# Attention weights turned by VectorE in 32x32 blocks and placed through DRAM, their normalisation on ScalarE

## The chip, the cores and the metric

One core of one Trainium2 chip runs the whole program. The metric is the device time of one execution in microseconds (us), smaller being better. The kernel before takes 1813.17 us (median of three runs, 1809.98 to 1820.33).

## What is computed

Two layers of a model on 256 latent tokens and 256 context tokens, width 2048, all in fp32. The first layer has 16 attention heads and 32 state-space heads beside each other (one input projection, one output projection); the second is a gated short convolution. Each layer is modulated by shift, scale and gate vectors, which are the product of a conditioning vector with a large matrix `ada_w`. The part that the change touches is the attention of one head:

```python
s_lat = jnp.einsum('bqhd,bkhd->bhqk', qr, kb).astype(jnp.float32) * scale + bias.astype(jnp.float32)
s_lat = jnp.where(mask, s_lat, -jnp.inf)
s_ctx = jnp.einsum('bqhd,bkhd->bhqk', qr, k_ctx).astype(jnp.float32) * scale
pr = jax.nn.softmax(jnp.concatenate([s_lat, s_ctx], axis=-1), axis=-1).astype(v.dtype)
return (jnp.einsum('bhqk,bkhd->bqhd', pr[..., :kh * GRID_W], vb)
        + jnp.einsum('bhqk,bkhd->bqhd', pr[..., kh * GRID_W:], v_ctx))
```

With 256 queries and 512 keys a head has 256x512 weights. They come out of the softmax with queries on the partitions, and the product with the values needs them with keys on the partitions, so they have to be turned.

## The kernel before, in words

**Weights.** Nearly all of the time goes into products with weight matrices, which are read from DRAM once. SP's queue loads them in tiles of 512 KB (L379, in `issue`) into five raw buffers, `raw_131` to `raw_135`. ACT casts a tile to its high part wH (L409, `split`), DVE forms the low part wL (L416, `low_part`) and thereby frees the raw buffer, and PE does three products for each tile (L198, `mm`). There are three pairs of wH and wL, so ACT can be three tiles ahead of PE at most, and SP five more. A tile is 24 matmuls of 512 columns in the input projection of keys, queries and the like, and 12 of 512 in the output projection.

**The order.** Python generators describe the work (one per head, per state-space group, per projection). A planner (`Plan`, L38) guesses what each instruction costs and, from the guesses, decides when a generator may issue its next step; every engine then runs its own list strictly in order. A changed cost guess, or a generator that holds a temporary buffer for longer, so moves instructions of other parts on all engines. There are ten temporary buffers of 128x512 (`tmp_104` to `tmp_113`), and a head reserves some with `grow` before it starts.

**An attention head** (`head_gen`, L992; 16 of them). Four DMAs of 64 KB on SP fetch the bias (L998). For each half of the queries (qt = 0, 1) PE forms the scores, one matmul of 128x512; DVE adds the bias and takes the maximum (L1013), ACT takes the exponential with its sum (L1018). DVE then forms the reciprocal of the sum (L1022) and multiplies the weights by it and by 0.5 (L1023). PE turns the weights, four transposes of 128x128 into a PSUM bank (`trans`, L1026 to 1028, through `turn`, L202), and ACT copies the bank to the tile PT (L1050). Four matmuls multiply with the values (L1058), DVE multiplies by the gate (L1062), and a DMA on ACT's queue writes the result to DRAM (L921). The two tiles PT_149 and PT_150 alternate between heads.

**Convolution of the state-space groups.** When the projection for B or C of a group is finished in its PSUM bank, ACT starts the convolution from that bank (L1169), DVE goes on with it, and ACT ends it with an activation (L1178).

**The modulation of the second layer** (`gemv_gen`, L787) is work in the background: 16 vectors of 512, and for each one eight tiles of `ada_w` of 512 KB, loaded by SP among the weights into the same raw buffers when one is to spare, and two multiply-adds on DVE for each (L803). The finished row goes by PE, DVE (L812) and a DMA on ACT's queue to DRAM (L815). When vector 11 is done, the twelve rows are read back by a DMA (L819), turned by PE and copied by DVE (L824); only then can `turn_gen` scale and turn the input of the second layer (L1556, L1568). The first matmul of the second layer needs that.

**The border of the layers.** The output projection ends with a multiply and an add on DVE for every bank (L1531, L1534, giving x1a and x1b); then follow a root mean square, transposes and the scaling, and the second layer's h (L1636 on ACT, L1617 on DVE).

**Completion of DMAs.** Eight completion counters go round among the DMAs of SP and of ACT: a DMA waits until the one eight before it has landed.

In the kernel after, a line from L988 to L1021 stands one line lower, and one behind `head_gen`'s middle nine lines lower: L1169 becomes L1178, L1178 becomes L1187, L1531 becomes L1540, L1534 becomes L1543, L1568 becomes L1577.

Of the kernel before, what the change touches and what calls it, by code (L numbers as in the profile page):

```python
# [11 lines left out]
ALU = mybir.AluOpType  # L12
# [25 lines left out]
class Plan:  # L38
# [32 lines left out]
    def cost(self, e, op, i, ins, outs):  # L71
        n = max(self.size(a) for a in ins + outs)
        if e == "PE":
            n, cols = self.size(outs[0]), outs[0].ap[0][1]
            if i.is_transpose:
                return n / 1.2 + 3, 190
            if ins[0].dtype == F32R:
                return 9 + 0.434 * n, 190
            return 2 * max(55, n / 1.2) * (0.27 if cols == 32 else 0.52 if cols == 64 else 1) + (80 if cols < 128 else 0), 190
        if e == "DVE":  # L80
            if op == "Memset":
                return n * 0.26 + 60, 90
            if op in ("Reciprocal", "TensorReduce"):
                return n * 1.04 + 70, 90
            if len([a for a in ins if self.size(a) >= n]) >= 2 or op == "ISA" or self.psum(ins):
                return n * 1.22 + 70, 90
            return n * 0.6 + 130, 90
        if e == "ACT":
            return n * 0.85 + 150 + (200 if len(outs) > 1 else 0), 100
        if e == "POOL":  # L90
            return (n * 186 if n < 70 else n * 2.4) + 150, 60
        return 60, 0
# [49 lines left out]
def kernel(ctx: ExitStack, tc, x, cx, ada_w, ada_b, w_in, w_out, sc_in, sc_out, rpb, small, const,  # L142
# [7 lines left out]
    V, S, G, T, DMA = nc.vector, nc.scalar, nc.gpsimd, nc.tensor, nc.sync  # L150
    DMA2 = nc.scalar
    plan = Plan()
    E = plan.add

    def st(shape, tag, dt=F32, name=None):
        return sb.tile(list(shape), dt, tag=tag, name=name or tag, bufs=1)
# [11 lines left out]
    def drt(shape, name):  # L168
        return dr.tile(list(shape), F32, name="dram_" + name)
# [3 lines left out]
    free_t = [st([128, 512], f"tmp{k}") for k in range(NTMP)]  # L173
    free_h = [st([128, 256], f"half{k}") for k in range(NHALF)]
    free_b = [pj.tile([128, 512], F32, tag=f"bank{k}", name=f"bank{k}", bufs=1) for k in range(8)]
# [4 lines left out]
    KT, QT, Vt, gt = st([128, 4, 512], "KT"), st([128, 4, 256], "QT"), st([128, 4, 512], "Vt"), st([128, 4, 256], "gt")  # L180
# [7 lines left out]
    def take(pool):  # L188
        b = min(pool, key=lambda a: plan.last[a.tensor.name])
        pool[:] = [a for a in pool if a is not b]  # L190
        return b

    tmp, half, raw_ = (lambda: take(free_t)), (lambda: take(free_h)), (lambda: take(free_r))
    two = lambda ap: ap.rearrange("p (a b) -> p a b", a=2)
    four = lambda ap: ap.rearrange("p (a b) -> p a b", a=4)

    def mm(o, l, r, start, stop):
        E(T.matmul(o, l, r, start=start, stop=stop, skip_group_check=True))  # L198

    def turn(o, i):  # L200
        k = i.shape[0]
        E(T.transpose(o, i, ident if k == 128 else ident[:k, :k]))  # L202
# [132 lines left out]
    def bank():  # L335
        return take(free_b)

    def give(pool, *bs):
        pool.extend(bs)

    W_ = lambda eng, *aps, nb=0: (eng, aps, nb)
# [577 lines left out]
    def put_mix(i, o):  # L919
        yield W_("AQ", o)  # L920
        E(DMA2.dma_start(mixd[i], o))  # L921
        give(free_h, o)
        written.add(i)
# [63 lines left out]
        got.add((key, a))  # L987

    b0 = rpbs[0, :, :]
    s4s = [st([128, 8], f"s4_{k}") for k in range(4)]  # L990

    def head_gen(a, h):  # L992
        hd = 4 * a + h
        bt, s4, P = bias[hd % 2], s4s[hd % 4], PT[hd % 2]
        yield when(lambda: hd < 2 or ("pv", hd - 2) in got)
        yield W_("SP")
        for r in range(4):
            E(DMA.dma_start(bt[64 * (r % 2):64 * (r % 2) + 64, r // 2, :].rearrange("p (a b) -> p a b", a=4),  # L998
                            bass.AP(tensor=b0.tensor, offset=b0.offset + hd * 64 * 320 + (7 - r) * 31 - 61,
                                    ap=[[319, 64], [31, 4], [1, 64]])))  # L1000
        yield W_("DVE", bt)
        bv = bt[:, 0:2, :].rearrange("p q (r c) -> p (q r) c", c=64)
        E(V.tensor_tensor(out=bv, in0=bv, in1=mask.unsqueeze(1).to_broadcast([128, 8, 64]), op=ALU.add))
        sps = {}

        def score(qt):
            ps = bank()
            mm(ps, QT[:, h, qt * 128:(qt + 1) * 128], KT[:, h, :], True, True)
            return ps

        def top(qt, ps):
            sp = sps[qt] = tmp()
            E(V.tensor_tensor_reduce(out=two(sp), in0=two(ps), in1=bt[:, 1:3, :] if qt else bt[:, 0::2, :], scale=1.0,  # L1013
                                     scalar=-3.0e38, op0=ALU.add, op1=ALU.max, accum_out=s4[:, qt:qt + 1]))
            give(free_b, ps)
            E(V.tensor_scalar(out=s4[:, 2 + qt:3 + qt], in0=s4[:, qt:qt + 1], scalar1=-1.0, scalar2=None, op0=ALU.mult))
            yield W_("ACT", sp, s4)
            E(S.activation(sp, sp, AF.Exp, bias=s4[:, 2 + qt:3 + qt], scale=1.0, accum_out=s4[:, 4 + qt:5 + qt]))  # L1018

        def scale_(qt):  # L1020
            sp = sps[qt]  # L1021
            E(V.reciprocal(s4[:, 6 + qt:7 + qt], s4[:, 4 + qt:5 + qt]))  # L1022
            E(V.tensor_scalar(out=sp, in0=sp, scalar1=s4[:, 6 + qt:7 + qt], scalar2=0.5, op0=ALU.mult, op1=ALU.mult))  # L1023

        def trans(qt):
            pt = bank()  # L1026
            for kt in range(4):
                turn(pt[:, kt * 128:(kt + 1) * 128], sps[qt][:, kt * 128:(kt + 1) * 128])
            give(free_t, sps[qt])
            return pt  # L1030

        yield when(lambda: ("K", a) in got and ("Q", a) in got)
        yield ("grow", 2, 0)
        yield W_("PE", KT[:, h, :], QT[:, h, :], nb=1)
        p0 = score(0)
        yield W_("DVE", p0)
        yield from top(0, p0)
        yield W_("PE", nb=1)
        p1 = score(1)
        yield W_("DVE", p1)  # L1040
        yield from top(1, p1)
        yield W_("DVE", sps[0])
        scale_(0)
        yield W_("DVE", sps[1])
        scale_(1)
        for qt in range(2):
            yield W_("PE", sps[qt], nb=1)
            pt = trans(qt)
            yield W_("ACT", pt)
            E(S.copy(P[:, :, qt * 128:(qt + 1) * 128], four(pt)))  # L1050
            give(free_b, pt)
        yield ("cap", 0, 0)
        yield when(lambda: ("V", a) in got and ("G", a) in got)
        yield ("grow", 0, 1)
        yield W_("PE", P, Vt, nb=1)
        po = bank()
        for kt in range(4):
            mm(po[:, :256], Vt[:, kt, h * 128:(h + 1) * 128], P[:, kt, :], kt == 0, kt == 3)  # L1058
        got.add(("pv", hd))
        yield W_("DVE", po)  # L1060
        o = half()
        E(V.tensor_tensor(out=o, in0=po[:, :256], in1=gt[:, h, :], op=ALU.mult))  # L1062
        give(free_b, po)
        attn[0] += 2
        yield from put_mix(hd, o)
# [381 lines left out]
    for h in range(4):  # L1447
        spawn(side, head_gen(0, h))
# [11 lines left out]
    def do_qk(a, nxt):  # L1460
        psQ = banks(2)
        proj(512, "act", psQ, 4)
        spawn(urgent, kq_gen("Q", a, psQ, 2, statq, QT, True), 2)
        psK = banks(4)
        proj(512, "act", psK, nxt)
        spawn(urgent, kq_gen("K", a, psK, 4, statk, KT, True), 4)
        for h in range(4):
            spawn(side, head_gen(a, h))
# [388 lines left out]
```

## Time and profile before

| what | value |
|---|---|
| median of three runs | 1813.17 us (1809.98 to 1820.33) |
| the profiled execution | 1814.06 us, its span 1812.3 us |
| granted clock of TensorE in that execution | 0.999 |
| busy | PE 98%, DVE 69%, ACT 43%, POOL 2% of the span |
| 16 DMA engines, queue q1 (SP's loads) | 63.8% of their span |

The profile is of one execution. "Busy" is the time in which an engine has an instruction running; PE is the matmul engine, DVE is VectorE, ACT is ScalarE, SP is the engine whose queue starts most of the DMAs. A group of instructions in the profile is a line of the kernel with its tiles and shape; "idle before" is how long the engine stood still ahead of such instructions, and what it waited for.

### The profile page before, as it was taken

The numbers are of one execution on the slowest core, as the hardware profiler recorded it, in microseconds if no ns is written. First come the engines' busy times: TensorE is split into PE (matmuls) and PEld (weight loads), VectorE is DVE, ScalarE is ACT, GpSimd is POOL, SyncE is SP. The second block draws the span as 40 slices with busy tenths as digits, with TensorE's granted clock in tenths as the row PEclk, the third lists the DMA queues.
The fourth block names the chain that finished last, engine by engine and source line by source line (L and its number), as shares of the span: only waits on it lengthen the run. The fifth ranks groups of instructions, "written<-read, shape, count | busy, mean of one in ns | idle before, by whom it ended". The sixth has DMA issues, their size and how long they took to land.

```text
span 1812.3 us, 26337 instructions
## 1 busy us (share of the span) xinstructions
PE 1775.1 (98%) x9961; PEld 1487.4 (82%) x9961; DVE 1259.2 (69%) x2041; ACT 775.3 (43%) x1362; POOL 30.5 (2%) x28
## 2 busy tenths in 40 slices
PE   5999999999999999999999999999999999999998
PEld 4677888888888888888888898778878888888887
DVE  5566875887575887575887687666667866665665
ACT  5422543455232455232454344544435444444442
POOL 0000100000000000000001000000000000000000
PEclk9999999999999999999999999999999999999999
DMA  9987654576655576655576566668776776666564
GB/s 337 342 289 254 196 163 135 169 217 202 204 168 168 170 220 198 218 165 169 170 221 186 165 185 185 205 211 300 268 248 203 241 231 188 190 192 188 192 211 153
DMA packets 249216, 376.90 MB, mean 208 GB/s; under 512 B 32656, under 2 KB 104048, under 8 KB 249088
## 3 DMA queue, kind: packets, MB, share of 16 engines
q1 hardware_dynamic: 239792, 366.64, 63.8%
q10 hardware_dynamic: 9296, 8.57, 1.4%
q8 instruction: 78, 1.28, 0.3%
q14 instruction: 50, 0.41, 0.1%
HBM read 368.70 MB, written 7.77 MB: 208 GB/s over the span
## 4 chain that ended last, share of the span: by engine, by line
PE 92%; DMA 3%; DVE 2%; issue 1%; ACT 1%; SPq 0%; POOL 0%; POOLq 0%; DVEq 0%; ACTq 0%
PE bank L198 90%; PE bank L202 3%; DMA raw<-in_ada_w 2%; DVE wL L416 1%; DVE acc L803 1%; DMA tmp<-dram_mixd 0%; DMA tmp<-dram_csr 0%; DVE hL L752 0%; SPq L566 0%; ACT wH L409 0%; DVE tmp L748 0%; ACT hH L746 0%; DVE xm L612 0%; ACT mix L1496 0%; DVE tmp L1790 0%
## 5 line engine op out<-in xcount | busy, mean ns | idle before, releaser
L409 ACT CAST wH<-raw 128x1024 fp32r<-128x1024 f32 (+1 forms) x440 | 459.0, 1044 | 701.2 <-PE bank L198 576.1
L416 DVE TENSOR_TENSOR wL<-raw,wH 128x1024 fp32r<-128x1024 f32 (+1 forms) x440 | 532.1, 1213 | 257.3 <-ACT wH L409 255.9
L198 PE MATMUL bank<-h,wH 128*128 128x512 f32 x1024 | 357.2, 395 | 2.7 <-ACT h L1636 1.5
L198 PE MATMUL bank<-hH,wH 128*128 128x256 f32 (+1 forms) x1040 | 352.6, 339 | 0.9 <-ACT wH L409 0.9
L198 PE MATMUL bank<-hL,wH 128*128 128x256 f32 (+1 forms) x1040 | 336.9, 324 | 0.0
L198 PE MATMUL bank<-hH,wL 128*128 128x256 f32 (+1 forms) x1024 | 331.2, 323 | 0.5 <-DVE wL L416 0.5
L198 PE MATMUL bank<-h,wL 128*128 128x256 f32 x1024 | 284.5, 278 | 0.0
L198 PE MATMUL bank<-wH,hH 128*128 128x512 f32 x640 | 257.4, 403 | 4.8 <-ACT hH L746 2.6
L198 PE MATMUL bank<-wL,hH 128*128 128x512 f32 x640 | 249.8, 391 | 0.3 <-DVE wL L416 0.3
L198 PE MATMUL bank<-wH,hL 128*128 128x512 f32 x640 | 249.3, 390 | 0.1
L803 DVE SCALAR_TENSOR_TENSOR acc<-raw,csil,acc 128x512 f32<-128x512 f32 x256 | 191.9, 750 | 65.5 <-DMA raw<-in_ada_w 52.0
L198 PEld LDWEIGHTS bank<-h,wH 128*128 128x128 f32 x1024 | 192.1, 188 | 49.1 <-issue 2.2
L198 PEld LDWEIGHTS bank<-hH,wH 128*128 128x128 f32 x1040 | 197.8, 190 | 23.2 <-issue 7.5
L198 PEld LDWEIGHTS bank<-hL,wH 128*128 128x128 f32 x1040 | 197.9, 190 | 19.8 <-issue 5.3
L198 PEld LDWEIGHTS bank<-hH,wL 128*128 128x128 f32 x1024 | 194.6, 190 | 16.5 <-DVE wL L416 1.1
L198 PEld LDWEIGHTS bank<-h,wL 128*128 128x128 f32 x1024 | 192.4, 188 | 0.0
L198 PE MATMUL bank<-wH,mix 128*128 128x512 f32 x512 | 164.1, 397 | 2.2 <-ACT wH L409 2.2
L198 PEld LDWEIGHTS bank<-wH,hH 128*128 128x128 f32 x640 | 120.2, 188 | 35.6 <-issue 7.5
L198 PEld LDWEIGHTS bank<-wH,hL 128*128 128x128 f32 x640 | 120.1, 188 | 25.4 <-DVE hL L752 0.6
L198 PEld LDWEIGHTS bank<-wL,hH 128*128 128x128 f32 x640 | 120.2, 188 | 24.3 <-DVE wL L416 1.1
L198 PEld LDWEIGHTS bank<-wH,mix 128*128 128x128 f32 x512 | 96.9, 189 | 23.4 <-ACT wH L409 2.7
L198 PE MATMUL bank<-wL,mix 128*128 128x512 f32 x256 | 100.6, 393 | 3.8 <-DVE wL L416 3.8
(244 smaller groups left out, 1662.9 us busy)
## 6 DMA issues: line engine op xcount, KB each, us to landing
raw<-in_w_in SPq DMA_DIRECT2D x209, 512.0 KB, 4.5
raw<-in_ada_w SPq DMA_DIRECT2D x163, 512.0 KB, 4.7
raw<-in_sc_in SPq DMA_DIRECT2D x128, 512.0 KB, 3.7
raw<-in_w_out SPq DMA_DIRECT2D x64, 512.0 KB, 4.3
raw<-in_sc_out SPq DMA_DIRECT2D x32, 512.0 KB, 4.5
tmp<-dram_csr SPq DMA_DIRECT2D x32, 256.0 KB, 7.1
PT<-in_ada_w SPq DMA_DIRECT2D x14, 512.0 KB, 5.8
yi<-in_ada_w SPq DMA_DIRECT2D x8, 512.0 KB
```

The costliest lines, as they stand in the source:

```text
L198: E(T.matmul(o, l, r, start=start, stop=stop, skip_group_check=True))
L202: E(T.transpose(o, i, ident if k == 128 else ident[:k, :k]))
L409: E(S.copy(H, v))
L416: E(V.tensor_tensor(out=Lo, in0=v, in1=H.bitcast(F32), op=ALU.subtract))
L803: E(V.scalar_tensor_tensor(out=acc, in0=v[:, j], scalar=csil[:, 2 * k + j:2 * k + j + 1], in1=acc, op0=ALU.mult, op1=ALU.add))
```

## The change

The reciprocal stays on DVE, but the multiplication by it moves to ACT (`S.mul`, L1026 after), and the factor 0.5 goes into the last multiplication by the gate. The four transposes by PE and the copy from PSUM are gone. In their place DVE turns every 32x32 block of the 128x512 weights where it stands (`V.transpose`, L1033 after, into another temporary buffer), four DMAs on SP's queue write the buffer to a new DRAM tile `ptd` in blocks (L1037 after: 64 KB each, 512 runs of 128 bytes), and when all eight of a head are written, one DMA on SP reads 512 KB back into the head's PT tile (L1044 after). A head reserves three temporary buffers instead of two, and the planner gets a cost guess for the new DVE instruction.

```diff
-            if op in ("Reciprocal", "TensorReduce"):
+            if op in ("Reciprocal", "TensorReduce", "StreamTranspose"):
...
+    ptd = drt([16, 512, 256], "ptd")
...
         def scale_(qt):
             sp = sps[qt]
+            yield W_("DVE", s4[:, 4 + qt:5 + qt])
             E(V.reciprocal(s4[:, 6 + qt:7 + qt], s4[:, 4 + qt:5 + qt]))
-            E(V.tensor_scalar(out=sp, in0=sp, scalar1=s4[:, 6 + qt:7 + qt], scalar2=0.5, op0=ALU.mult, op1=ALU.mult))
-
-        def trans(qt):
-            pt = bank()
-            for kt in range(4):
-                turn(pt[:, kt * 128:(kt + 1) * 128], sps[qt][:, kt * 128:(kt + 1) * 128])
+            yield W_("ACT", s4[:, 6 + qt:7 + qt])
+            E(S.mul(sp, sp, s4[:, 6 + qt:7 + qt]))
+
+        pd = ptd[hd]
+
+        def blocks(qt):
+            yield W_("DVE", sps[qt])
+            tb = tmp()
+            E(V.transpose(tb, sps[qt]))
             give(free_t, sps[qt])
-            return pt
+            yield W_("SP", tb)
+            for a_ in range(4):
+                E(DMA.dma_start(bass.AP(tensor=ptd.tensor, offset=pd.offset + qt * 128 + a_ * 32,
+                                        ap=[[256, 32], [8192, 16], [1, 32]]),
+                                tb[32 * a_:32 * a_ + 32].rearrange("p (b j) -> p b j", j=32)))
+            give(free_t, tb)
+
+        def fetch():
+            yield W_("SP", pd)
+            E(DMA.dma_start(P, pd.rearrange("(k p) q -> p k q", p=128)))
...
-        yield ("grow", 2, 0)
+        yield ("grow", 3, 0)
...
-        yield W_("DVE", sps[0])
-        scale_(0)
-        yield W_("DVE", sps[1])
-        scale_(1)
         for qt in range(2):
-            yield W_("PE", sps[qt], nb=1)
-            pt = trans(qt)
-            yield W_("ACT", pt)
-            E(S.copy(P[:, :, qt * 128:(qt + 1) * 128], four(pt)))
-            give(free_b, pt)
+            yield from scale_(qt)
+        for qt in range(2):
+            yield from blocks(qt)
         yield ("cap", 0, 0)
+        yield from fetch()
...
-        E(V.tensor_tensor(out=o, in0=po[:, :256], in1=gt[:, h, :], op=ALU.mult))
+        E(V.scalar_tensor_tensor(out=o, in0=po[:, :256], scalar=0.5, in1=gt[:, h, :], op0=ALU.mult, op1=ALU.mult))
```

The planner, fed with other instructions, also writes other parts in another order. Three places matter for what follows.

**SP, last pair of heads.** SP's list after, in the output projection: raw_ are weight tiles, tmp_ to dram_ptd the blocks, PT_ the read back.

```order
L379 DMA raw_132<-in_w_out 128x2x512
L379 DMA raw_131<-in_w_out 128x2x512
L1037 DMA dram_ptd<-tmp_108 32x16x32 x4
L1037 DMA dram_ptd<-tmp_105 32x16x32 x4
L1037 DMA dram_ptd<-tmp_111 32x16x32 x4
L1044 DMA PT_149<-dram_ptd 128x4x256
L379 DMA raw_133<-in_w_out 128x2x512
L1037 DMA dram_ptd<-tmp_106 32x16x32 x4
L379 DMA raw_135<-in_ada_w 128x2x512
L379 DMA raw_134<-in_w_out 128x2x512
```

Before, nothing but weights and `ada_w` stands in these places; now the weight tile `raw_133` stands behind twelve block DMAs and a read back, and the next one behind four more. At the first pair of heads all sixteen block DMAs and a read back stand ahead of the next weight.

**ACT, the end of a group's C projection.** ACT's list before, around the convolution (L1169) of the second group; half_ is C of the group, and the bank it reads is filled by the last matmul of the C projection. wH_136 and wH_137 are the first two tiles of the X projection, which follows on PE.

```order
L409 CAST wH_136<-raw_132 128x1024
L409 CAST wH_137<-raw_135 128x1024
L1178 ACTIVATE tmp_106<-tmp_104 128x512
L1204 COPY Bl<-tmp_105 128x256
L1210 COPY Btmt<-bank_129 128x512
L409 CAST wH_138<-raw_131 128x1024
L1169 ACTIVATE half_119<-bank_130,cbh,cwh 128x256
```

The same place after, where L1169 is L1178; the first two tiles of the X projection are again wH_136 and wH_137.

```order
L1178 ACTIVATE half_116<-bank_127,cbh,cwh 128x256
L409 CAST wH_136<-raw_131 128x1024
L1213 COPY Bl<-tmp_109 128x256
L1219 COPY Btmt<-bank_130 128x512
L1213 COPY Bl<-tmp_112 128x256
L1219 COPY Btmt<-bank_129 128x512
L1187 ACTIVATE half_122<-half_116 128x256
L1178 ACTIVATE half_115<-bank_127,cbh,cwh 128x256
L1187 ACTIVATE half_121<-half_115 128x256
L409 CAST wH_137<-raw_134 128x1024
```

The casts of the first two tiles stood ahead of the convolution that waits for the last matmul of C; now they stand behind it. The third group has the same order.

**DVE, the border of the layers.** DVE's list before, from the last bank of the output projection to the first h of the second layer.

```order
L1531 TENSOR_TENSOR tmp_109<-bank_130,tmp_109 128x512
L1534 TENSOR_TENSOR x1b<-tmp_109,tmp_113 128x512
L1598 TENSOR_SCALAR r_9145<-ss_9143,s_9146 128x1
L1604 TENSOR_SCALAR half_121<-const,r_9145 128x128
L1629 TENSOR_TENSOR PT_149<-PT_149,bank_125 128x256 x2
L1617 SCALAR_TENSOR_TENSOR h_0_10456<-PT_149,M_218,h_0_10456 128x256
```

The same stretch after, where lines stand nine lower; M_218 is the modulation of the second layer.

```order
L1540 TENSOR_TENSOR tmp_113<-bank_128,tmp_113 128x512
L1543 TENSOR_TENSOR x1b<-tmp_113,tmp_108 128x512
L803 SCALAR_TENSOR_TENSOR acc<-raw_133,csil,acc 128x512
L1607 TENSOR_SCALAR r_9086<-ss_9084,s_9087 128x1
L803 SCALAR_TENSOR_TENSOR acc<-raw_133,csil,acc 128x512
L1613 TENSOR_SCALAR half_119<-const,r_9086 128x128
L803 SCALAR_TENSOR_TENSOR acc<-raw_133,csil,acc 128x512 x4
L812 COPY rowb<-bank_130 128x128
L824 COPY M_218<-bank_125 128x32
L1565 SCALAR_TENSOR_TENSOR A_9085<-M_218,small 128x16
L1638 TENSOR_TENSOR PT_149<-PT_149,bank_123 128x256 x2
L1626 SCALAR_TENSOR_TENSOR h_0_10392<-PT_149,M_218,h_0_10392 128x256
```

The last three tiles of vector 11 of the modulation (six L803, through the one buffer raw_133), its row and the copy of M_218 now stand between the end of the output projection and the second layer. Before, the copy of M_218 (L824) stands 226 rows above x1b in DVE's list, among the last heads and state-space groups.

## The prediction

> **What bounds the kernel now.** I read the busy times first, then the slices, then the chain that ended last. From the page of the kernel before:
>
> ```profile
> PE 1775.1 (98%) x9961; PEld 1487.4 (82%) x9961; DVE 1259.2 (69%) x2041; ACT 775.3 (43%) x1362; POOL 30.5 (2%) x28
> PE   5999999999999999999999999999999999999998
> DVE  5566875887575887575887687666667866665665
> DMA  9987654576655576655576566668776776666564
> PE 92%; DMA 3%; DVE 2%; issue 1%; ACT 1%; SPq 0%; POOL 0%; POOLq 0%; DVEq 0%; ACTq 0%
> PE bank L198 90%; PE bank L202 3%; DMA raw<-in_ada_w 2%; DVE wL L416 1%; DVE acc L803 1%; DMA tmp<-dram_mixd 0%; DMA tmp<-dram_csr 0%; DVE hL L752 0%; SPq L566 0%; ACT wH L409 0%; DVE tmp L748 0%; ACT hH L746 0%; DVE xm L612 0%; ACT mix L14
> ```
>
> PE is busy 98% of the span and in full use in 38 of 40 slices; the matmuls with weights (L198) are 90% of the chain, and PE's transposes (L202) 3%. So work taken off PE shortens the run directly, and any wait put in front of PE lengthens it directly. DVE is busy five to eight tenths of each slice and the DMA engines mostly five to seven, so both have room on average. The loads have it too, by what SP waits for:
>
> ```profile
> SPq L379 <- DVE wL L416: 815.3, 333, 13.3
> ```
>
> In 333 loads SP stands still until DVE has freed a raw buffer: weights arrive before they are wanted, by up to five tiles of cover. The times below go against the profiled execution, 1814.06 us (span 1812.3 and 1.8 around it); the median of the runs lies 0.9 lower, and I take that off at the end.
>
> **Term 1, the transposes leave PE.** A group of four transposes in PE's timeline, between products of 512 columns (columns: start, duration, engine, line, what):
>
> ```profile
> 274.22 0.39 PE L198 MATMUL bank<-hL,wH 128*128 128x512 f32 x1
> 274.44 0.40 PE L198 MATMUL bank<-hH,wL 128*128 128x512 f32 x1
> 274.69 0.60 PE L202 MATMUL bank<-const,tmp 128*128 128x128 f32 x4
> 275.04 0.48 PE L198 MATMUL bank<-hH,wH 128*128 128x512 f32 x1
> 275.36 0.40 PE L198 MATMUL bank<-hL,wH 128*128 128x512 f32 x1
> ```
>
> Two products start 0.22 to 0.23 us apart when nothing stands between them. From 274.44 to 275.36 there are two steps of product and one group: 0.92 less 0.46 leaves 0.46 us for the group. There are 16 heads with two groups: 32 x 0.46 = **14.7 us** less. The lower bound is the 0.35 us between the starts alone (11.2 us); the upper one the first row of the next view, 45.6 us for 324 transposes, 128 of which go (18.0 us). I take the middle, since it is what the neighbours lose.
>
> Other groups of the same view, by line and shape (busy in all, mean of one in ns, idle time ahead):
>
> ```profile
> L202 PE MATMUL bank<-const,tmp 128*128 128x128 f32 x324 | 45.6, 272 | 0.2 <-ACT KT L962 0.2
> L1050 ACT COPY PT<-bank 128x512 f32<-128x512 f32 x32 | 18.0, 589 | 36.0 <-PE bank L202 34.7 <-DMA dram_csr<-tmp 1.3
> L1023 DVE TENSOR_SCALAR tmp<-tmp,s 128x512 f32<-128x512 f32 x32 | 15.6, 487 | 1.1
> L596 ACT ACTIVATE xs<-xs,rx 128x512 f32<-128x512 f32 x8 | 5.5, 717 | 6.9 <-POOL rx L555 6.9
> L1062 DVE TENSOR_TENSOR half<-bank,gt 128x256 f32<-128x256 f32 x16 | 6.8, 424 | 30.7 <-PE bank L198 30.7
> L1303 DVE SCALAR_TENSOR_TENSOR yi<-tmp,small,tmp 128x256 f32<-128x256 f32 x16 | 7.8, 485 | 0.6
> ```
>
> ACT loses the copy L1050 (589 ns) and gets a multiplication from SBUF to SBUF, priced by L596 (717 ns): 32 x 0.13 = 4 us more on an engine with 57% idle. DVE loses L1023 (487 ns) and gets the block turn, which the trace does not show: no less than those 487 ns, no more than the 1222 ns of a row of twice the size (L416 below); I take 0.7, as 512 columns with two inputs take there. That is 7 us on DVE spread over 16 heads, and L1062 becomes like L1303, 485 for 424 ns. All of this stands beside PE's matmuls and costs nothing by itself; if DVE had no room, the bound would be 32 x 0.7 = 23 us. What the turn triggers costs more.
>
> **Term 2, the casts behind the convolution.** Durations from the same view:
>
> ```profile
> L409 ACT CAST wH<-raw 128x1024 fp32r<-128x1024 f32 x433 | 454.8, 1051 | 683.4 <-PE bank L198 564.4 <-issue 89.4 <-DMA raw<-in_w_out 6.9
> L416 DVE TENSOR_TENSOR wL<-raw,wH 128x1024 fp32r<-128x1024 f32 x433 | 527.3, 1222 | 256.7 <-ACT wH L409 255.2
> L1169 ACT ACTIVATE half<-bank,cbh,cwh 128x256 f32<-128x256 f32 x8 | 4.5, 557 | 1.0 <-PE bank L198 1.0
> ```
>
> Before, the cast of the first tile of X stood ahead of the convolution of C and was long done. Now PE ends C's last matmul, ACT works 0.56 us at L1169, then 1.05 us at the cast: PE waits 1.6 us. It has two products with the high part (0.46 us) while DVE forms the low part (1.22 us): 0.8 more. The next cast stands behind seven ACT rows of which one waits for DVE's convolution, and I lay those against the 5.5 us (24 x 0.2275) of the tile in work: about 0.8 and 0.8 again. That is 4.0 us for a place, and it stands in the second and the third group: **8 us**, between 0 (if the projection is late on another engine anyway) and 9.
>
> **Term 3, weights behind the blocks.** What a small DMA takes on SP (L998, 64 KB in runs of 256 bytes), and how long DMAs take to land:
>
> ```profile
> L998 SPq DMA_DIRECT2D bias<-dram_rpbs x64: 573/615/641, 230.2 to 1170.1; - x64
> ...
> DMA to landing us min/median/max: 2.4/3.1/3.9
> ```
>
> ```profile
> raw<-in_ada_w SPq DMA_DIRECT2D x163, 512.0 KB, 4.7
> raw<-in_w_out SPq DMA_DIRECT2D x64, 512.0 KB, 4.3
> dram_mixd<-half ACTq DMA_DIRECT2D x32, 128.0 KB, 2.7
> ```
>
> ```profile
> q10 hardware_dynamic: 9296, 8.57, 1.4%
> ```
>
> At the last pair SP has 12 block DMAs (12 x 0.615 = 7.4 us) and a read back, which waits until the last block has landed (2.7 us as for L921's write of 128 KB), before weight raw_133; that lands 4.3 us later and is cast in 1.05: 15.9 us with the issues. In the output projection a tile is 12 products, 2.73 us, and five loaded tiles cover 13.7: PE waits some 2.2, then 0.8 for the low part, and again 2.8 at the next tile, which stands behind four more blocks: 5.8. The first pair has 16 blocks (9.8 us), a read back and a wait for a completion counter ahead of the weight, but tiles of 5.46 us; a bit over 4 us. The six pairs between have fewer blocks in a row, or longer tiles: 0 to 1.5 each, 2 in all by my reading. Sum **12 us**. This rests on a block's time in the queue, which no row shows: 512 runs of 128 bytes are 32 for each of 16 engines. Queue q10, which writes 0.92 KB a packet, has 1.4% of 16 x 1812.3 us for 9296 packets, 44 ns each: 1.4 us for a block if a short packet is no cheaper, 0.2 us if it goes by bytes. I take 0.7, at about the issue. At 0.2 the issue (0.615) still sets the pace and the term stays near 10; at 1.4 each block is 0.7 longer, 16 of them 11 us at each of the two tight pairs, and the term is about 35. Below nothing it can't be, since the blocks only add.
>
> The page "DMA: Bandwidth & Descriptors" of the Trainium skill, section "Specifications", says that a transfer under 512 bytes is below line rate because the DMA engine then reads, modifies and writes; it speaks against this change. By that rule a packet would cost at least the 44 ns and perhaps twice, and the term would be 35 us and more. No row shows a write so short, so no run yet bears on it.
>
> **Term 4, the border of the layers.** The modulation of the second layer, when its row goes to DRAM and comes back (count, min/median/max in ns, first and last start):
>
> ```profile
> L812 DVE COPY rowb<-bank x16: 280/291/293, 279.5 to 1481.8; 128x128 f32<-128x128 f32 x16
> L815 ACTq DMA_DIRECT2D dram_mrow<-rowb x16: 483/502/1028, 281.5 to 1484.0; - x16
> L819 ACTq DMA_DIRECT2D rowb<-dram_mrow x1: 333/333/333, 1098.4 to 1098.4; - x1
> L202 PE MATMUL bank<-const,rowb x1: 243/243/243, 1111.7 to 1111.7; 32*128 32x32 f32 x1
> ```
>
> ```profile
> L803 DVE SCALAR_TENSOR_TENSOR acc<-raw,csil,acc 128x512 f32<-128x512 f32 x256 | 191.9, 750 | 65.5 <-DMA raw<-in_ada_w 52.0 <-issue 5.7 <-DMA acc<-in_ada_b 2.9
> ```
>
> L819 runs at 1098.4 us, and the rows are turned at 1111.7. The border itself, by three timelines:
>
> ```profile
> 1354.92 0.69 DVE L1534 TENSOR_TENSOR x1b<-tmp,tmp 128x512 f32<-128x512 f32 x1
> ```
>
> ```profile
> 1358.61 0.91 ACT L1636 ACTIVATE h<-PT,M 128x256 fp32r<-128x256 f32 x2 [2.24 <-DVE PT L1629]
> ```
>
> ```profile
> 1359.69 0.50 PE L198 MATMUL bank<-h,wH 128*128 128x512 f32 x1 [0.92 <-DVE h L1617]
> ```
>
> x1b is done at 1355.61, and the second layer's first product starts 4.1 us later. So the modulation had 240 us to spare, and the change uses all of it up: since temporary and raw buffers are held longer and DVE's list is fuller, DVE's copy of the modulation slips by 226 rows of its list, and the `ada_w` tiles with it, until three are left at the border. They go through one raw buffer: two L803 (1.5 us), load (4.7), 1.5, load (4.7), 1.5: 13.9 us. Then PE's sum (0.5), L812 (0.3), the write L815 (2.7 as for L921, less than 128 KB though), the read L819 (2.7), turn and copy (0.5), A (0.2), eight scalings on ACT at 0.4 (3.0), and about 0.9 to the first h: 24.7 us instead of 4.1. The loads meet an empty queue and the first two L803 fall into waits of L1607, so I take **18 us** more (bounds 12, if loads land in 3 us and DMAs in 2, and 21).
>
> Small waits on DVE that move from place to place add **1 us**.
>
> **The sum.** -14.7 + 8 + 12 + 1 + 18 = +24.3 us; 1838.4 on the profiled execution, 1837.5 against the median. I forecast **1837 us**, 1.3% slower.
>
> **The rivals.** A measurement of this kernel can tell about 0.5% from no change, 9 us: under 1804.1 is faster, over 1822.2 slower.
> - *The transposes are all that counts* (faster). PE is 98% busy and its waits are short; if the planner's order hides the modulation's tiles (they come ahead of the border because SP has time to spare) and the casts are late by less than the cover, only term 1 and some 3 us remain: 1802. For it: SP's 815 us of waiting. Against it: six L803 and the copy of M_218 stand behind x1b in a list that DVE follows in order. It decides when terms 2 to 4 are under 5.6 us together. 6%.
> - *Half of it* (within 0.5%). The border costs its 18 and the rest is hidden, or the other way round: -14.7 + 18 = 1817. 12%.
> - *Blocks clog the queue* (slower by far). At 2 us a block SP's queue loses 16 x 1.3 = 21 us more at each of eight pairs; the two tight pairs pay all of it, the six others what is over about 10 us of cover: 2 x 21 + 6 x 11 = 108, so 1945. For it: no row has runs of 128 bytes; against it: L998's runs of 256 bytes land in 3.1 us and PE runs on. Between 0.7 and 2 us every time up to there is possible. 16%.
> - *The forecast*, 1822 to 1860: 66%.
>
> The range goes from 1815 (half of it) to 1880 (blocks at 1.2 us, and the upper bounds of the other terms); some 10% lie on each side. Faster 0.06, same 0.12, slower 0.82.
>
> **What would show it.** In the profile after: L202 with 196 instead of 324 transposes and PE's busy time about 15 us lower; PE's idle time ahead of L198 put down to ACT wH L409 in two places of about 4 us (term 2); SP's list with block DMAs landing in 2 to 3.5 us, and DVE's turn at about 0.7 us a time; at the border, some 22 us from x1b to the first h, with L803, L815 and L819 in it. Landings over 5 us for a block would speak for the clogged queue. A modulation read back (L819) long before the border would show term 4 wrong, and with it the sign would be open.

## The result, and the profile after

The changed kernel takes **1839.95 us**, the median of four runs (1838.42 to 1844.91); the kernel before, beside it on the same chip, 1814.90 (1809.98 to 1820.33). The ratio is **1.0141 [1.0116, 1.0165]**: 1.4% slower. The profiled execution took 1839.92 us, with a span of 1838.1; against the profiled one of before that is 25.9 us more.

The page after: busy times, PE's slices, the clock granted to PE, and the chain that ended last.

```profile
PE 1778.1 (97%) x9833; PEld 1484.9 (81%) x9833; DVE 1262.0 (69%) x2041; ACT 779.1 (42%) x1362; POOL 31.4 (2%) x28
...
PE   6999998999999999999999999999969999999998
...
PEclk9999999999999999999999999999979999999999
...
PE 83%; DVE 7%; DMA 5%; ACT 2%; issue 1%; SPq 1%; POOL 0%; ACTq 0%; DVEq 0%
```

PE issues 128 matmuls fewer, as it should, and yet is busy 3.0 us longer, so its matmuls have become slower; the prediction had looked for some 15 us less. One slice, the 30th, has a hole in it; the clock has one in the same place. PE's part of the chain falls from 92% to 83%. What PE lost went to DVE, the loads, ACT and SP.

The groups of the changed part, by line and shape:

```profile
L202 PE MATMUL bank<-const,tmp 128*128 128x128 f32 x196 | 29.2, 280 | 0.2 <-ACT KT L962 0.2
L1033 DVE STREAM_TRANSPOSE tmp<-tmp 128x512 f32<-128x512 f32 x32 | 22.1, 703 | 10.1 <-DMA dram_ptd<-tmp 5.4 <-ACT tmp L1026 4.6
L1026 ACT ACTIVATE tmp<-tmp,s 128x512 f32<-128x512 f32 x32 | 22.1, 717 | 5.9 <-DVE s L1024 5.6
```

128 transposes are gone. DVE turns a 128x512 buffer in 703 ns, and ACT multiplies one in 717 ns. Both are as the prediction priced them, and both stand beside the matmuls.

**The border of the layers**, on DVE. This is its timeline from the end of the output projection to the modulation:

```profile
1355.81 0.69 DVE L1543 TENSOR_TENSOR x1b<-tmp,tmp 128x512 f32<-128x512 f32 x1
...
1362.02 1.54 DVE L803 SCALAR_TENSOR_TENSOR acc<-raw,csil,acc 128x512 f32<-128x512 f32 x2 [3.12 <-DMA raw<-in_ada_w]
1367.41 1.54 DVE L803 SCALAR_TENSOR_TENSOR acc<-raw,csil,acc 128x512 f32<-128x512 f32 x2 [3.85 <-DMA raw<-in_ada_w]
1369.73 0.29 DVE L812 COPY rowb<-bank 128x128 f32<-128x128 f32 x1 [0.78 <-PE bank L198]
1374.85 0.19 DVE L824 COPY M<-bank 128x32 f32<-128x32 f32 x1 [4.83 <-PE bank L202]
```

And PE at the same place:

```profile
1354.31 0.39 PE L198 MATMUL bank<-wH,mix 128*128 128x512 f32 x1
...
1369.01 0.65 PE L198 MATMUL bank<-acc,const 128*32 128x128 f32 x8 [7.98 <-DVE acc L803]
1374.53 0.28 PE L202 MATMUL bank<-const,rowb 32*128 32x32 f32 x1 [4.87 <-DMA rowb<-dram_mrow]
...
1380.57 0.47 PE L198 MATMUL bank<-h,wH 128*128 128x512 f32 x1
```

The tile `rowb` says when the twelve rows were read back:

```profile
L819 ACTq DMA_DIRECT2D rowb<-dram_mrow x1: 333/333/333, 1372.7 to 1372.7; - x1
```

The chain stands as forecast: two tiles of `ada_w` through one raw buffer, the sum on PE, L812, the row to DRAM and back (L819 at 1372.7 instead of 1098.4), and the copy of M. From PE's last product with `mix` to the first product with h it is 1380.57 - 1354.31 = 26.26 us. Before, the same two products start at 1353.45 and 1359.69:

```profile
1353.45 0.39 PE L198 MATMUL bank<-wH,mix 128*128 128x512 f32 x1
...
1359.69 0.50 PE L198 MATMUL bank<-h,wH 128*128 128x512 f32 x1 [0.92 <-DVE h L1617]
```

That is 6.24 us. So the border costs **20.0 us** more. Up to the last product with `mix` the changed kernel is only 0.9 us behind, and from the first product with h to the end it loses 5.0 more: 0.9 + 20.0 + 5.0 = 25.9.

**Ahead of the border** the transposes' gain is lost in short waits. The place of the casts, second group; ACT, DVE and PE in order of start:

```profile
538.31 0.56 ACT L1178 ACTIVATE half<-bank,cbh,cwh 128x256 f32<-128x256 f32 x1 [1.49 <-PE bank L198]
538.78 1.03 ACT L409 CAST wH<-raw 128x1024 fp32r<-128x1024 f32 x1
...
539.84 1.23 DVE L416 TENSOR_TENSOR wL<-raw,wH 128x1024 fp32r<-128x1024 f32 x1 [3.01 <-ACT wH L409]
...
539.86 0.50 PE L198 MATMUL bank<-hH,wH 128*128 128x512 f32 x1 [1.59 <-ACT wH L409]
...
541.12 0.51 PE L198 MATMUL bank<-hH,wL 128*128 128x512 f32 x1 [0.53 <-DVE wL L416]
```

The cast starts when the convolution L1178 is through, and PE waits 1.59 us for it, then 0.53 for the low part. The third group has the same two waits at 812.38 and 813.64. The next tile has none.

The same stretch by windows (columns: window, its length, busy time and instructions of PE, PEld, DVE, ACT and POOL, PE's granted clock, DMA share, GB/s), of the kernel after:

```profile
300.00:325.00 25.00, 20.23 (x127) 17.92 (x126) 22.42 (x36) 11.50 (x17) 0.00 (x0) 0.93 0.49 128
540.00:560.00 20.00, 19.35 (x81) 15.69 (x82) 14.22 (x22) 6.63 (x11) 0.00 (x0) 0.91 0.64 207
542.00:547.00 5.00, 5.00 (x21) 4.22 (x20) 3.87 (x9) 2.37 (x6) 0.00 (x0) 0.70 0.77 243
```

and before:

```profile
300.00:325.00 25.00, 25.00 (x164) 22.94 (x163) 17.41 (x24) 11.62 (x17) 0.00 (x0) 1.00 0.45 137
540.00:560.00 20.00, 20.00 (x93) 16.55 (x92) 14.58 (x22) 6.92 (x11) 0.00 (x0) 1.00 0.65 210
```

From 542 to 547 PE is busy all the time, and has 0.70 of its clock: 1.5 us more are lost there, after the wait is over. In the trace's clock records this is one stretch of 3.4 us at half clock, from 541.6; the third group has another from 814.6. The prediction had no such term.

At the first pair of heads, PE, then ACT and DVE:

```profile
302.29 0.39 PE L198 MATMUL bank<-hH,wH 128*128 128x256 f32 x1 [1.42 <-ACT wH L409]
...
306.14 0.58 PE L198 MATMUL bank<-hH,wL 128*128 128x256 f32 x1 [3.35 <-DVE wL L416]
```

```profile
301.21 1.98 ACT L409 CAST wH<-raw 128x1024 fp32r<-128x1024 f32 x2
```

```profile
298.38 4.53 DVE L1184 SCALAR_TENSOR_TENSOR tmp<-bank,cwh,tmp 128x510 f32<-128x510 f32 x6
...
304.87 2.35 DVE L416 TENSOR_TENSOR wL<-raw,wH 128x1024 fp32r<-128x1024 f32 x2
```

PE is idle 4.8 us here. ACT's cast shows no wait for a load, and DVE comes to the low part straight from nine rows of the convolution: the lists are in a worse order, and no weight landed late. SP had issued the last weight before this place by 289.7 us.

SP, ACT and PE at the last pair:

```profile
1197.14 7.88 SPq L1037 DMA_DIRECT2D dram_ptd<-tmp  x12
1205.19 0.38 SPq L1044 DMA_DIRECT2D PT<-dram_ptd  x1
1205.62 0.52 SPq L379 DMA_DIRECT2D raw<-in_w_out  x1
```

```profile
1211.33 1.05 ACT L409 CAST wH<-raw 128x1024 fp32r<-128x1024 f32 x1 [5.77 <-DMA raw<-in_w_out]
```

```profile
1218.99 0.50 PE L198 MATMUL bank<-wL,mix 128*128 128x512 f32 x1 [0.54 <-DVE wL L416]
```

The twelve blocks and the read back stand ahead of the weight and take 8.5 us of the queue, and the weight does land late: ACT stands idle 5.77 us for it, until 1211.33. But PE loses only 0.29 us for it, at 1213.69, and 0.54 at 1218.99: from the first block on it had work for 16.3 us. Between 300 us and the last product with `mix` PE is idle 15.9 us after and 6.1 before; two of before's waits are the following, which are gone after:

```profile
1157.18 0.49 PE L198 MATMUL bank<-wH,mix 128*128 128x512 f32 x1 [2.23 <-ACT wH L409]
1159.41 0.56 PE L198 MATMUL bank<-wL,mix 128*128 128x512 f32 x1 [1.75 <-DVE wL L416]
```

### The profile page after: what moved, and what is told of

The parts are those of the page before. It is cut to its first block, busy times and chain, and to the rows that moved or that the text cites. A ratio compares the mean times of both kernels' runs of the same rounds, so it can differ in the third digit from the quotient of the medians.

```text
span 1838.1 us, 26255 instructions
## 1 busy us (share of the span) xinstructions
PE 1778.1 (97%) x9833; PEld 1484.9 (81%) x9833; DVE 1262.0 (69%) x2041; ACT 779.1 (42%) x1362; POOL 31.4 (2%) x28
## 4 chain that ended last, share of the span: by engine, by line
PE 83%; DVE 7%; DMA 5%; ACT 2%; issue 1%; SPq 1%; POOL 0%; ACTq 0%; DVEq 0%
PE bank L198 81%; DMA raw<-in_ada_w 3%; DVE wL L416 2%; PE bank L202 2%; DMA raw<-in_w_in 1%; ACT wH L409 1%; DVE tmp L1184 1%; DVE acc L803 1%; DMA raw<-in_w_out 1%; SPq L1037 1%; DVE half L1184 0%; DVE tmp L1365 0%; DMA bias<-dram_rpbs 0%; DMA xs<-in_x 0%; DVE mix L1506 0%
## 5 line engine op out<-in xcount | busy, mean ns | idle before, releaser
L198 PE MATMUL bank<-h,wH 128*128 128x512 f32 x1024 | 361.6, 398 | 0.9 <-ACT h L1645 0.6
L803 DVE SCALAR_TENSOR_TENSOR acc<-raw,csil,acc 128x512 f32<-128x512 f32 x256 | 191.6, 748 | 59.4 <-DMA raw<-in_ada_w 52.9
```

Source lines behind the costliest of these rows:

```text
L803: E(V.scalar_tensor_tensor(out=acc, in0=v[:, j], scalar=csil[:, 2 * k + j:2 * k + j + 1], in1=acc, op0=ALU.mult, op1=ALU.add))
```

## The experiments

Theory A: the change saves PE about 14 us and costs more by where the planner then puts things: above all the modulation at the border, and casts behind convolutions. The rivals: B, the short writes to DRAM load the DMA queues, so that whatever is behind them lands late; C, the multiplication on ACT costs; D, the transposes were worth less than thought. The kernel before was run beside each: 1815.9 us with the first four, 1816.9 with the others.

**The background taken earlier.** The planner's third number says how far ahead of PE background work may be taken; from 2000 on, two further restrictions on it fall away too.

```diff
-    HOR = ((urgent, 4500.0), (side, 2500.0), (back, 1500.0))
+    HOR = ((urgent, 4500.0), (side, 2500.0), (back, 2500.0))
```

> The changed kernel, with one number of the planner changed: background work may be issued up to 2500 ns ahead of PE by the planner's clock instead of 1500. In the list of DVE the copy of the modulation of the second layer (L824) then stands far ahead of the border again, with no L803 between the output projection and the second layer. Theory (the border costs about 18 us, the blocks themselves little): 1816 to 1823 us, 17 to 24 under the changed kernel, with L819 long before the border. Rival one (the blocks and their read back clog SP's queue): the border is not where the time is, 1835 to 1842. Rival two (any order costs the same, since PE then waits elsewhere): 1835 to 1842 with the border short and new waits ahead of it.

Measured: 1813.89 us (1811.51 to 1815.81), ratio 0.9990 [0.9975, 1.0005]. The tile `rowb`:

```profile
L819 ACTq DMA_DIRECT2D rowb<-dram_mrow x1: 333/333/333, 1237.4 to 1237.4; - x1
```

The read back is 135 us earlier, and from the last product with `mix` to the first with h it is again 6.27 us, within 0.03 of before. The whole kernel gains 26 us over the changed one, 2 more than the expected range reached: the 20.0 of the border and, in the profile, 5.9 of waits ahead of it. The border is **shown** to be the largest part of the loss. This kernel is even with the one before: it is 5.0 us ahead at the last product with `mix`, and loses 5.5 in the second layer.

**The same number in the kernel before**, as a control.

> The kernel before, with only the planner's number of the first experiment changed (background work up to 2500 ns ahead instead of 1500). It is the control for that experiment. Theory (the modulation was on time in the kernel before, so there is nothing to gain): 1812 to 1820, within 0.3% of the kernel before. Rival (the number by itself is worth something, whatever the transposes): 1795 to 1808.

Measured: 1822.04 us, ratio 1.0025 [1.0014, 1.0035], 2 us above the expected range. The number by itself is no improvement; it makes the kernel before 0.25% slower, and in the changed kernel it mends what the change put at the border. With the number in both, the changed kernel is some 0.35% the faster (0.9990 to 1.0025).

**The transposes doubled**, in the kernel before: every group of four is done twice.

```diff
-            for kt in range(4):
+            for kt in (0, 1, 2, 3, 0, 1, 2, 3):
```

> The kernel before, with every group of four transposes by PE done twice into the same bank (same result). Theory (a group costs PE 0.46 us): 32 x 0.46 = 14.7 us more, 1825 to 1832 against 1815. Rival one (the transposes fill gaps of PE and cost nothing): 1815. Rival two (the busy time of a transpose as its row gives it, 0.141 us each): 18 us more, 1833.

Measured: 1828.79 us, ratio 1.0075 [1.0056, 1.0095]: 13.6 us more (10.2 to 17.3). The group, by line:

```profile
L202 PE MATMUL bank<-const,tmp 128*128 128x128 f32 x452 | 59.3, 272 | 0.2 <-ACT KT L962 0.2
```

128 transposes more are 13.7 us of busy time (59.3 less 45.6). D falls: 32 groups are worth their 14 us. This is another plan too: up to the last product with `mix` the profiled execution is 9.7 us later, with 3.1 us less of waits after 300 us and without the one stretch at half clock (1.7 us) of the kernel before. That leaves 14.5 for the transposes, so 13.6 is good to about 1 us.

**The multiplication on ACT alone**, in the kernel before; PE still turns the weights.

```diff
-            E(V.tensor_scalar(out=sp, in0=sp, scalar1=s4[:, 6 + qt:7 + qt], scalar2=0.5, op0=ALU.mult, op1=ALU.mult))
+            yield W_("ACT", s4[:, 6 + qt:7 + qt])
+            E(S.mul(sp, sp, s4[:, 6 + qt:7 + qt]))
...
-        E(V.tensor_tensor(out=o, in0=po[:, :256], in1=gt[:, h, :], op=ALU.mult))
+        E(V.scalar_tensor_tensor(out=o, in0=po[:, :256], scalar=0.5, in1=gt[:, h, :], op0=ALU.mult, op1=ALU.mult))
```

> The kernel before, with only one part of the change: the normalisation multiplies on ACT and the factor 0.5 goes into the multiplication by the gate; the transposes by PE and the copy from PSUM stay. Theory (ACT and DVE have room): no change, 1812 to 1819. Rival (the way over ACT, 0.72 us in its list between casts, delays the casts that PE waits for): 4 to 10 us more.

Measured: 1816.64 us, ratio 1.0013 [0.9997, 1.0029]. No difference; C falls.

**Every block written twice**, the second time to a DRAM tile that nothing reads.

```diff
...
+                E(DMA.dma_start(bass.AP(tensor=ptx.tensor, offset=pd.offset + qt * 128 + a_ * 32,
+                                        ap=[[256, 32], [8192, 16], [1, 32]]),
+                                tb[32 * a_:32 * a_ + 32].rearrange("p (b j) -> p b j", j=32)))
```

> The changed kernel, with each of the 128 block DMAs done twice, the second into a DRAM tile that nothing reads. Theory (blocks cost little in the queue, but the planner counts them, and the modulation of the second layer slips further): the output projection ends within 10 us of where it ends in the changed kernel, and the border takes 25 to 30 us more, 1860 to 1878 in all. Rival one (128-byte runs clog the queue): 128 more blocks of 0.7 us or more ahead of weights, 40 us or more ahead of the border. Rival two (the DMA is free and the order stays): 1840.

Measured: 1885.51 us, ratio 1.0382 [1.0357, 1.0407], 7 us above the expected range. DVE and PE at the border:

```profile
1376.19 1.54 DVE L803 SCALAR_TENSOR_TENSOR acc<-raw,csil,acc 128x512 f32<-128x512 f32 x2 [0.87 <-DMA acc<-in_ada_b]
1381.67 1.54 DVE L803 SCALAR_TENSOR_TENSOR acc<-raw,csil,acc 128x512 f32<-128x512 f32 x2 [3.94 <-DMA raw<-in_ada_w]
...
1414.27 1.54 DVE L803 SCALAR_TENSOR_TENSOR acc<-raw,csil,acc 128x512 f32<-128x512 f32 x2 [3.88 <-DMA raw<-in_ada_w]
```

```profile
1415.87 0.66 PE L198 MATMUL bank<-acc,const 128*32 128x128 f32 x8 [39.34 <-DVE acc L803]
```

Now all eight tiles of the vector, 5.45 us apart, stand at the border, which costs 49.9 us over before (20.0 after the change). Ahead of it the kernel is 17.7 us behind before, 16.9 more than the changed kernel, where at most 10 were expected: 0.13 us for each of the 128 further DMAs. A clogged queue (B) would have taken a good deal more ahead of the border, 1.3 us a block at two pairs alone being 42. What more DMAs cost is again mostly the place of the modulation: 29.9 of the 46.

**One write for a buffer**, in rows of 2 KB: 32 writes instead of 128. This kernel leaves out the placing of the blocks, so what it reads back is not the turned matrix; everything else is done.

```diff
-            for a_ in range(4):
-                E(DMA.dma_start(bass.AP(tensor=ptd.tensor, offset=pd.offset + qt * 128 + a_ * 32,
-                                        ap=[[256, 32], [8192, 16], [1, 32]]),
-                                tb[32 * a_:32 * a_ + 32].rearrange("p (b j) -> p b j", j=32)))
+            E(DMA.dma_start(bass.AP(tensor=ptd.tensor, offset=pd.offset + qt * 65536, ap=[[512, 128], [1, 512]]), tb))
```

> The changed kernel, with one DMA for each 128x512 buffer instead of four, in rows of 2 KB: 32 writes instead of 128, the same bytes, DVE's turn, the read back and the wait for it as in the changed kernel. It leaves out the placing of the blocks: they lie in DRAM in rows as they come. Theory (what costs is the number of DMAs in SP's list, which the planner spaces and which stand ahead of weights; the transposes by PE are really saved): the modulation is back long before the border and the waits ahead of it mostly go, 1798 to 1806, 0.5 to 1% faster than the kernel before. Rival one (the way through DRAM costs as such: latency of write and read back): 1815 to 1830. Rival two (the border stays as it is): 1830 or more.

Measured: 1795.61 us, ratio 0.9878 [0.9862, 0.9894], below the expected range. The tile `rowb`:

```profile
L819 ACTq DMA_DIRECT2D rowb<-dram_mrow x1: 350/350/350, 1102.3 to 1102.3; - x1
```

With the planner's number as in the changed kernel, the modulation is back where it was, and the border costs 0.02 us. Between 300 us and the last product with `mix` PE is idle only 1.2 us, and the kernel is 22.0 us ahead of before there. So the block DMAs bring both the waits and the border. Run length and number change together in this run. The border can't come from the run length: the planner charges every DMA 450 ns of SP's time and then its bytes (L109 to L115), whatever its runs, and its order is fixed before the kernel runs. What it also does, in its own clock, is to put a write behind the landing of the one before to the same stretch of DRAM, and by its reckoning (`keys`, L50) the eight interleaved block writes of a head overlap, while the two of this run don't. No run parts the number from this overlap, nor the queue's time from the plan in what the waits cost.

**The cast ahead of the convolution.** In the changed kernel, the convolution waits until the next tile's cast has been issued:

```diff
+        yield when(lambda: pos["split"] >= pos["use"] + 1)
         yield W_("ACT", ps)
```

> The changed kernel, with one condition: the convolution's first step may go into ACT's list only when the cast of the next weight tile stands there already. At the two places of the prediction's second term the cast then stands one row ahead of the convolution that waits for the last matmul of C; PE's list stays the same but for single rows. Theory (PE waits for the cast there, 1.6 us, and some more for the low part): the 1.6 us of ACT wH L409 at these places go, the low part's wait stays or grows, 2 to 4 us less than the changed kernel, 1835 to 1838. Rival one (the whole 8 us of the term go, with the slower clock behind each wait): 1830 to 1833. Rival two (the convolution then comes later and PE waits for that): 1840 or more.

Measured: 1838.27 us, ratio 1.0115 [1.0098, 1.0132]; this interval overlaps that of the changed kernel, so no gain is shown; the expected range ended at 1838. PE, second group:

```profile
538.43 0.51 PE L198 MATMUL bank<-hH,wL 128*128 128x512 f32 x1 [0.52 <-DVE wL L416]
...
545.28 0.50 PE L198 MATMUL bank<-hH,wH 128*128 128x512 f32 x1 [0.70 <-ACT wH L409]
...
547.55 0.50 PE L198 MATMUL bank<-hH,wL 128*128 128x512 f32 x1 [1.54 <-DVE wL L416]
```

The wait of 1.59 us is gone, and 0.70 and 1.54 stand at the next tile; the third group shows the same (0.69 and 1.53). The wait moved. That ACT and DVE have as much to do as before would explain it, which is argued and not shown. Mending one step of the order is not worth its cost term.

**Six DMAs a head**, complete: two writes in rows of 2 KB, four read backs that place the blocks, and the background number of the first experiment.

```diff
+            E(DMA.dma_start(bass.AP(tensor=ptd.tensor, offset=pd.offset + qt * 65536, ap=[[512, 128], [1, 512]]), tb))
...
+            for b_ in range(4):
+                E(DMA.dma_start(P[32 * b_:32 * b_ + 32].rearrange("p k (a j) -> p k a j", j=32),
+                                bass.AP(tensor=ptd.tensor, offset=pd.offset + b_ * 32,
+                                        ap=[[512, 32], [128, 4], [16384, 8], [1, 32]])))
```

> A full version with six DMAs a head instead of nine: each buffer is written in rows of 2 KB by one DMA, and four DMAs of 128 KB read a head back, each 32 partitions in runs of 128 bytes, so that the placing is done by the reads; and background work up to 2500 ns ahead. Theory: the gain of the transposes is kept and the new waits mostly go: 1798 to 1808. Rival one (reads in runs of 128 bytes are slow, 1024 runs each, and the weights behind them are late): 1815 to 1850. Rival two (nothing gained over the first experiment): 1812 to 1818.

Measured: 1807.33 us (1805.91 to 1808.13), ratio **0.9943 [0.9929, 0.9957]**: faster than both kernels. Its runs of 128 bytes are as many as in the changed kernel, only read instead of written, in 96 DMAs in all instead of 144. The gain of the transposes arrives: it is 15.1 us ahead of before at the border, of which 6.8 are left in the profiled run's end. Beside the first experiment, which has the same number of the planner and nine DMAs a head, it is 6.6 us faster.

## Why the prediction was right

The time (1837 forecast, 1839.95 measured) and the sign were right, and the largest term came about as described. That the total came within 3 us is in part luck: the waits were put 6.5 us too high, the border 2.0 too low, and 5.0 were not foreseen.

- **Term 1, the transposes: right.** Forecast 14.7 (11.2 to 18), measured 13.6 by the doubling. The prices of the turn (0.7) and of ACT's multiplication (717 ns) were right, and the multiplication alone costs nothing.
- **Term 2, the casts: the places right, the make-up wrong.** The two waits of the first tile are there, 1.59 and 0.53 us for 1.6 and 0.8. The second tile's, 0.8 and 0.8, did not appear. In their place PE ran on at a lower clock: 1.5 us in 5 us. A place comes to 3.6 us, for a forecast of 4.0.
- **Term 3, weights behind the blocks: the step that failed.** The prediction made the last pair the worst place, 5.8 us, by a weight that lands late behind twelve blocks; PE lost 0.8 there. The landing was forecast well: 14.2 us after the first block, for 14.9, although the read back did not wait the 2.7 us for the last block (it reads the head whose eight blocks stand first, and starts right behind the twelfth). The cover was wrong: 13.7 us for five loaded tiles left out the tiles that were cast already, and PE had work for 16.3. The first pair lost 4.8, for "a bit over 4", but by ACT's and DVE's order and not by a landing; that the size agrees is luck. Queue q1's row before and after:

```profile
q1 hardware_dynamic: 239792, 366.64, 63.8%
```

```profile
q1 hardware_dynamic: 315824, 383.43, 68.1%
```

  0.681 x 16 x 1838.1 less 0.638 x 16 x 1812.3 is 1528 us of one engine, 95 of all sixteen, for 128 blocks and their 16 read backs. The 65536 packets of 128 bytes are 51 of these 95: the trace has them at 12.5 ns each on the mean, so a block is 0.40 us of the sixteen engines, for 0.7 assumed. SP's issue, 0.66 us a block (12 in 7.88), was the slower of the two and set the pace. Taken in the order of their issue, the packets of a block were done 2.7 us after it in the median (1.3 to 6.5, five of 128 over 5 us), where the prediction looked for 2 to 3.5; the queue was not clogged. The page "DMA: Bandwidth & Descriptors" of the Trainium skill, section "Specifications", has the DMA engine read, modify and write below 512 bytes. In the packets' times no such cost shows, 12.5 ns for 128 bytes beside 21.2 for 256, and the 35 us and more that the prediction gave the term by that rule did not come.
- **Terms 2 and 3 and the small waits together.** Forecast 21. The profile has 0.9 us net ahead of the border, so with 13.6 saved the waits cost 14.5. Their make-up: PE idles 15.9 us after 300 us instead of 6.1, and 1.4 less ahead of it: 8.4. The rest, 6.1, fits the clock: the trace's clock records have five stretches of 3.4 us at half clock ahead of the border after (from 306.0, 388.0, 541.6, 814.6 and 958.0) and one before (from 1159.7), 1.7 us each, 6.8 net. The prediction set the waits too high by not taking off those of before, which go, and left the clock out.
- **Term 4, the border: right.** Forecast 18 (12 to 21), measured 20.0, and taken away whole by the first experiment. The loads did not meet the empty queue as well as hoped: 1362.02 to 1367.41 is 5.4 us a tile. Of the transposes that followed, the first ones ran at half clock, which the prediction left out here too.
- **Not foreseen: 5.0 us in the second layer.** PE waits for nothing there, but its products take longer. By line, before and after:

```profile
L198 PE MATMUL bank<-h,wH 128*128 128x512 f32 x1024 | 357.2, 395 | 2.7 <-ACT h L1636 1.5 <-DVE h L1617 1.2
```

```profile
L198 PE MATMUL bank<-h,wH 128*128 128x512 f32 x1024 | 361.6, 398 | 0.9 <-ACT h L1645 0.6 <-DVE h L1626 0.2
```

  From one product of 512 columns to the next it is 235.3 ns on the mean after and 232.7 before; this 1.1% of 450 us is the 5.0. The multiplication on ACT alone (4.0 us more in that layer), the kernel before with the other number (4.3) and all other variants of the changed kernel lose there too (3.7 to 5.5, the six DMAs 8.3, of which 2.5 are waits of PE); the doubled transposes (0.4) don't. The loss does not go with blocks, border or loads of `ada_w`. It may belong to the execution and not to the kernel: one of each is profiled, and those of the kernel before alone spread from 1808.88 to 1827.79 us. Its cause is **open**.

Sum: -13.6 + 14.5 + 20.0 + 5.0 = +25.9, for -14.7 + 21 + 18 = +24.3 forecast. The 14.5 is what the other terms leave, so the sum itself is no test; that idle time and clock give 15.2 for it is one.

Of the rivals, *the transposes are all that counts* failed because all three other losses are real; *half of it* because both halves came; *blocks clog the queue* by the price above and the doubled blocks. The prediction missed a cause behind terms 2 to 4: it priced the blocks one by one in SP's queue, and what decided, for the border at least, was the order that the planner makes of them. One write per buffer removes the waits and the border at once; for the waits it stays open how much of that is the order and how much the queue.

## What to carry to other kernels

Work taken off the busiest engine is worth its full time there, here 0.43 us for a group of four transposes, but only if the way round doesn't displace background work that a later stage needs: look in the new order for what slides to the border between stages. Where transfers are issued one by one, and a planner orders the rest by its guesses of them, count the DMAs before the bytes: six a head instead of nine, with the same short runs on the other side of DRAM, and the background let go earlier, turned 1.4% slower into 0.6% faster. Count as cover all that lies between a load and its use, the tiles already cast included. A cast moved ahead of one wait brought nothing, since the wait came back one tile later.

## What the runs showed of the hardware

**A wait can cost PE more than its length.** After waits of 1.59 and 0.53 us the granted clock was 0.70 in the next 5 us, with PE fully busy. Not every wait does this: in the run with the cast ahead, the second group's waits of 0.52, 0.70 and 1.54 us left it at 1.00 from 540 to 560. At the border, after long waits, the transposes start 0.21 us apart at first, and later 0.11:

```profile
1375.01 0.42 PE L202 MATMUL bank<-const,x1b 128*128 128x128 f32 x1
1375.23 0.42 PE L202 MATMUL bank<-const,x1a 128*128 128x128 f32 x1
...
1378.03 0.27 PE L202 MATMUL bank<-const,x1a 128*128 128x128 f32 x1
1378.14 0.27 PE L202 MATMUL bank<-const,x1b 128*128 128x128 f32 x1
```

The clock is 0.50 from 1374.7 to 1377.8, about 3 us after work resumes, and 1.00 from 1378.0 to 1380.5. The page "TensorE: Matmul & The Clock Gate" of the Trainium skill, section "Part 1: The HAM clock gate (the "warmup" mystery)", has the half clock after an idle window of some 3.4 us, and the full one after as long a busy one. The 3 us of slow transposes agree; that waits of 1.59 and 0.53 us were enough does not.

**Two speeds at a granted clock of 1.00.** In the second layer, stretches in which products with h start 231 ns apart stand beside others with 236 or 237, at the same granted clock. How much of the layer has the slower one decides the 5.0 us above. No run here shows what sets them.
